# The two-input arithmetic of GpSimd goes to VectorE in a two-layer transformer trunk, and relu squared reads one factor from PSUM

## The chip, the cores and the metric

The kernel runs on one core of one Trainium2 chip. The metric is the device time of one execution in microseconds (us); lower is better. The engines are TensorE (PE), VectorE (DVE), ScalarE (ACT), GpSimd (POOL) and SyncE (SP, which here only issues DMAs). Each engine works through its own instruction stream in order, and waits on semaphores for the others.

## The reference

One sequence of 512 tokens with 1024 columns goes through two layers, all in fp32. A layer is, cut to what matters:

```
h = rmsnorm(x, norm_mix);  proj = h @ w_in                    # q, k, v, gates, u of three mixers
y_a = nsa_attention(...)   # 8 heads: compressed, full and window branches
y_b = banded_attention(...)  # window attention with sinks
y_c = s5_layer(u, ...)     # scan of a diagonal complex state, then gelu and a gate
merged = sum_i sigmoid(g_i) * (y_i @ w_branch_i)
x = x + merged @ w_out
h = rmsnorm(x, norm_mlp)
x = x + square(relu(h @ w_mlp_up)) @ w_mlp_down               # 4096 hidden columns
```

After the second layer one more rmsnorm gives the output.

## The kernel before

**Products in two parts.** Every fp32 operand of a large product is kept as a high part and a low part in the format fp32r, and a product is three matmuls: high by high, high by low, low by high (`mm3`, lines 143 to 145; `proj_tok`, line 563). A piece of weights (128 x 1024, 512 KB) is loaded by SP into `wr` (two buffers). `split` makes the two parts (three buffers each): ACT copies `wr` to the high part `wh` (line 136), and then VectorE or GpSimd subtracts to get the low part `wl` (line 137). Which of the two does it is the argument `eng`, None for VectorE.

**The stages of a layer.** The projections come first (with the first norm and the tables of the scan in layer 0), then the scan itself (`s5_quarter`, four quarters of 8 groups), then the attention, then the merge, `w_out`, and the MLP. In the attention the softmax work of one unit stands between the products of the unit before, and a generator `fill` feeds gate and branch products to TensorE in between. The MLP has four rounds (`fc`): eight up tiles (8 x 24 matmuls, one piece of weights each), then two column halves of the down product (four pieces each). For an up tile ACT takes the relu from its PSUM bank into `rel` (line 1348), VectorE squares it (line 1349), ACT copies the high part `ah` and VectorE subtracts the low part `al` (line 1350).

**The scan's tables.** `s5_prep` computes, by quarters, two tables with powers (`powers`, lines 497 to 499: a product on VectorE into `wpn` or `mo`, a product on GpSimd into `wpnt` or `mot`, and their sum on VectorE), the phasors `E`, and small matmuls (line 528) whose results VectorE adds into `ed` (line 532). The tables of layer 0 are made during its projections, those of layer 1 during the MLP of layer 0 (`steps` in `mlp`). The MLP of layer 1 has no such work beside it.

**Who sets the order.** The code states what depends on what and in which order things are wanted; a scheduling layer below it sets each engine's stream from that and from its own estimate of durations. So where an instruction stands changes when another one goes to another engine, and not only at the changed lines.

**GpSimd's arithmetic before.** The weights' low parts of layer 0's three first projections and of its whole MLP; those of the pieces that `fill` loads in both layers; one product of each table; the products with the sine and the back rotation in the scan (lines 741 and 749); the sums `merged` in `fill` (line 839); and the power -0.5 of each norm (line 230). GpSimd also issues the DMAs that store and load the scan's tables.

Of the kernel before, what the change touches and what calls it, by code (L numbers as in the profile page):

```python
# [28 lines left out]
# columns of the constant array  # L29
# [31 lines left out]
def bcast_rows(ap1d, n):  # L61
    """[n] in DRAM -> [128, n], the same row on every partition."""
    return bass.AP(tensor=ap1d.tensor, offset=ap1d.offset, ap=[[0, 128], [1, n]])


class Trunk:
# [14 lines left out]
    @contextmanager  # L81
    def after(self, pins):
        """What is emitted inside stays behind the given instructions in their engines' order."""
        with ExitStack() as s:
            for i in pins:
                s.enter_context(self.tc.issue_after(i.ins))
            yield

    # ---------------------------------------------------------------- background work
    def spawn(self, gen, delay=1):  # L90
        """Work cut into steps, set between the steps of the main line; a step yields how many of those to let pass."""
        item = [delay, gen]
        self.bg.append(item)
        return item
# [18 lines left out]
    # ---------------------------------------------------------------- psum  # L113
# [9 lines left out]
    # ---------------------------------------------------------------- weights  # L123
# [23 lines left out]
    # ---------------------------------------------------------------- constants  # L147
# [14 lines left out]
    def reduce_angle(self, pool, ang, n, name):  # L162
        """ang -> ang - 2 pi round(ang / 2 pi), in place."""
# [12 lines left out]
    def sincos(self, pool, ang, n, cos, sin, name):  # L176
        """cos and sin of ang in [-pi, pi]; ang is used up."""
# [28 lines left out]
    # ---------------------------------------------------------------- norm  # L206
    def norm_begin(self, p, row):
        """RMSNorm of self.x in two column halves: gain and the parts that a token tile takes."""
# [4 lines left out]
    def norm_sum(self, t, c, a=0, z=512):  # L213
        """Mean square of a token tile, after columns a to z of its half c are final (in their order)."""
# [32 lines left out]
    def norm_T(self, t):  # L247
        """Token tile t of the norm, transposed, in its two parts."""
# [4 lines left out]
    def norm_last(self, xg):  # L253
        """The norm of the last token tile, to be transposed by last_turn amid the work that follows."""
# [3 lines left out]
    def last_tile(self, b, mm, xg):  # L258
        """The last token tile's last columns in two parts, and its norm, brought out in the shortest time."""
# [32 lines left out]
    def first_norm(self, pa):  # L292
        """The first norm by token tiles, as a function that brings one up to its place in self.h, and the first
        pieces of weights that are loaded between the tiles."""
# [13 lines left out]
        # the tensor engine's clock rises only under load: keep it busy while the first tiles come  # L308
# [38 lines left out]
    # ---------------------------------------------------------------- S5 parameters  # L347
    def s5_init(self, l, p):
        """Powers of the discretised state matrix and its unit phasors, all groups at once."""
# [18 lines left out]
        # unit phasors of 8 * 2^k tokens, and of one  # L368
# [21 lines left out]
        # powers a^(8-e), e = 0..8  # L390
# [11 lines left out]
        # |a|^8  # L402
# [3 lines left out]
        # discretisation coefficient  # L406
# [17 lines left out]
    def s5_prep(self, l, init=None):  # L424
        """Tables of the chunked S5 scan (chunks of 8 tokens), by quarters of 8 groups, to DRAM."""
# [5 lines left out]
        with tc.tile_pool(name="prep", bufs=1, side="right", reuse_waits="tile") as p:  # L431
            pins.enter_context(self.after(self.pins))
            PR, PI, co_r, co_i, GC, GS, T1, T2, cmul = init[0] if init else list(self.s5_init(l, p))[1]
            # phasors of 8 b and of 64 a tokens, a, b < 8
# [12 lines left out]
            # the sine, which the imaginary half takes with the other sign  # L447
# [16 lines left out]
            for q in range(4):  # L464
# [8 lines left out]
                # B and C with their signs  # L473
# [15 lines left out]
                # tables with powers  # L489
                s4 = [128, 8, 8, 16]  # L490

                def powers(u, e0, name, sign=OP.add):
# [5 lines left out]
                    nc.gpsimd.tensor_tensor(tm, u2, pi, op=OP.mult)  # L498
# [4 lines left out]
                # phasors of the 64 chunks  # L503
# [18 lines left out]
                # the input table, transposed, and K[l] of the 8 lags, with d on lag 0  # L522
# [16 lines left out]
    # ---------------------------------------------------------------- projections to [token, column]  # L539
    def proj_tok(self, h, src, n, evac, stride=False, eng=None, lead=None, pre=()):  # L540
# [8 lines left out]
        for kp, t in order:  # L549
# [9 lines left out]
            # the low parts of the weights come last  # L559
# [8 lines left out]
    def resident(self, pool, src, n=4):  # L568
        """Pieces that all stay, as lists of [128, 512] parts per row tile."""
# [18 lines left out]
    def rope(self, pool, ps, t, out, shape):  # L588
        """ps [128, *heads, 64] -> rotated into out [128, *heads(, dup), 64]."""
# [14 lines left out]
    # ---------------------------------------------------------------- mixers  # L604
# [66 lines left out]
    def s5_u(self, l, h, p):  # L671
# [8 lines left out]
        self.proj_tok(h, self.I["wu"][l], 512, evac_u, stride=True, eng=None if l else self.nc.gpsimd)  # L680
# [21 lines left out]
    def s5_quarter(self, l, q, z, p):  # L702
        """The scan of 8 groups, over chunks of 8 tokens, up to the GLU's input."""
# [12 lines left out]
        # U[(s, h), group, chunk]  # L716
# [10 lines left out]
        # chunk inputs, rotated, scanned, rotated back  # L727
# [13 lines left out]
        nc.gpsimd.tensor_tensor(B, B, sinS, op=OP.mult)  # L741
# [4 lines left out]
        # the state before each chunk  # L746
        nc.gpsimd.memset(A[:, :, 0:1], 0.0)
        for k in (0, 64):
            nc.gpsimd.tensor_tensor(B[k:k + 64, :, 0:63], G[64 - k:128 - k, :, 0:63], sinS[64 - k:128 - k, :, 0:63], op=OP.mult)  # L749
# [17 lines left out]
    def glu(self, l, z, p):  # L767
# [14 lines left out]
        # the output takes the place of z  # L782
        for ct in range(4):
# [5 lines left out]
            # columns are (7 - j, c) of token 8 c + j  # L789
# [7 lines left out]
    def fill(self, l, h, yc, yb, merged, p, ng):  # L797
        for ct in range(ng, KT):
            yield from self.gate_first(l, 2, ct, h, merged, self.nc.gpsimd)
        yield from self.merge(l, 2, h, yc, merged, p, True, eng=self.nc.gpsimd)  # L800
# [256 lines left out]
    def b_parts(self, l, p, yb, t, hg):  # L1057
# [4 lines left out]
        P = []  # L1062
# [406 lines left out]
```

## Time and profile before

| | |
|---|---|
| median of 3 runs | 1933.46 us (1932.26 to 1934.83) |
| span of the profiled execution, first to last instruction | 1921.7 us |
| what lies around the span, against the median of the runs | 11.8 us |
| PE busy, share of the span | 1788.5 us, 93% |
| VectorE busy | 1156.1 us, 60% |
| ScalarE busy | 788.4 us, 41% |
| GpSimd busy | 428.4 us, 22% |

The profile is one execution on the chip. For it no time but its span is given; the three timed runs stand 11.8 us above that span at their median. Busy time is a mean over stages that have different limits, so each stage is read by itself. PE's busy time comes from modelled ends of matmuls; the granted clock says what share of the full TensorE clock was given.

### The profile page before, as it was taken

What the parts mean: (1) busy time and instruction counts of PE and PEld (TensorE: products, weight loads), DVE (VectorE), ACT (ScalarE), POOL (GpSimd) and SP (SyncE); (2) the same over time, 40 slices, a digit from 0 to 9 for tenths busy, and PEclk for the clock granted to TensorE, in tenths of its full rate; (3) what the DMA queues carried; (4) which work ended last, traced back from release to release, by engine and by line L of the source; (5) the groups of instructions that cost most, each with busy time, mean ns of one, the idle gap of its engine ahead of it and who ended that gap; (6) DMA issues with size and microseconds to landing.
All of it is one profiled execution on the core that took longest, in us unless ns stands there. A gap on an engine that the chain in (4) does not pass through costs nothing.

```text
span 1921.7 us, 23301 instructions
## 1 busy us (share of the span) xinstructions
PE 1788.5 (93%) x8560; PEld 1474.9 (77%) x8560; DVE 1156.1 (60%) x2552; ACT 788.4 (41%) x1575; POOL 428.4 (22%) x261
## 2 busy tenths in 40 slices
PE   7787989889999988989999999999899999999998
PEld 5776777677888866777787988777778888888887
DVE  7895558999345746355356456799954454334344
ACT  4422357666233323222334433776643333323232
POOL 4333421121202355455420032221230000000000
PEclk8898999999999999999999999999999999999999
DMA  5336421110333233333335353111132413333222
GB/s 165 112 131 178 143 68 56 33 45 23 134 102 119 64 102 107 119 110 109 123 110 158 111 154 110 55 45 34 34 109 90 141 59 96 99 99 99 94 95 86
DMA packets 66802, 188.23 MB, mean 98 GB/s; under 512 B 17984, under 2 KB 19168, under 8 KB 66688
## 3 DMA queue, kind: packets, MB, share of 16 engines
q1 hardware_dynamic: 57072, 156.53, 25.3%
q0 software_dynamic: 8320, 25.76, 4.4%
q10 hardware_dynamic: 1296, 4.46, 0.6%
q8 instruction: 67, 1.10, 0.2%
q14 instruction: 47, 0.39, 0.1%
HBM read 168.93 MB, written 17.76 MB: 97 GB/s over the span
## 4 chain that ended last, share of the span: by engine, by line
PE 59%; DVE 15%; issue 10%; POOL 4%; ACT 3%; DMA 1%; POOLq 0%; ACTq 0%; DVEq 0%
PE b_mm L144 16%; PE b_mm L145 16%; PE b_mm L143 16%; PE b_mm L563 3%; DVE aP L1212 3%; PE b_t L890 2%; POOL wl L137 1%; DVE ptl L897 1%; DVE aP L1199 1%; PE b_y L1121 1%; PE b_y L1119 1%; DVE rel L1349 1%; POOL sB L749 1%; POOL wpnt L498 1%; ACT wh L136 1%
## 5 line engine op out<-in xcount | busy, mean ns | idle before, releaser
L136 ACT CAST wh<-wr 128x1024 fp32r<-128x1024 f32 (+1 forms) x244 | 254.6, 1044 | 504.5 <-PE b_mm L144 233.4
L137 POOL TENSOR_TENSOR wl<-wr,wh 128x1024 fp32r<-128x1024 f32 (+1 forms) x112 | 276.2, 2468 | 541.5 <-ACT wh L136 426.8
L143 PE MATMUL b_mm<-hh,wh 128*128 128x512 f32 (+2 forms) x928 | 361.7, 390 | 0.5 <-ACT hh L290 0.5
L144 PE MATMUL b_mm<-hl,wh 128*128 128x512 f32 (+2 forms) x928 | 361.0, 389 | 0.6 <-DVE hl L290 0.6
L145 PE MATMUL b_mm<-hh,wl 128*128 128x512 f32 (+2 forms) x928 | 359.6, 387 | 0.3 <-POOL wl L137 0.3
L137 DVE TENSOR_TENSOR wl<-wr,wh 128x1024 fp32r<-128x1024 f32 (+1 forms) x132 | 164.6, 1249 | 281.4 <-ACT wh L136 281.2
L144 PEld LDWEIGHTS b_mm<-hl,wh 128*128 128x128 f32 x928 | 175.9, 190 | 33.4 <-DVE hl L290 1.1
L143 PEld LDWEIGHTS b_mm<-hh,wh 128*128 128x128 f32 x928 | 175.9, 190 | 33.1 <-ACT hh L290 1.0
L145 PEld LDWEIGHTS b_mm<-hh,wl 128*128 128x128 f32 x928 | 175.6, 189 | 33.2 <-POOL wl L137 1.2
L144 PE MATMUL b_mm<-wl,ah 128*128 128x512 f32 x448 | 176.0, 393 | 10.0 <-POOL wl L137 10.0
L143 PE MATMUL b_mm<-wh,ah 128*128 128x512 f32 x448 | 175.3, 391 | 0.0
L145 PE MATMUL b_mm<-wh,al 128*128 128x512 f32 x448 | 175.2, 391 | 0.0
L586 DVE TENSOR_TENSOR x<-b_mm,x 128x512 f32<-128x512 f32 x79 | 53.7, 688 | 114.2 <-PE b_mm L145 113.5
L563 PE MATMUL b_mm<-wh,hh 128*128 128x512 f32 (+1 forms) x320 | 108.6, 419 | 9.8 <-ACT v L982 4.7
L563 PE MATMUL b_mm<-wh,hl 128*128 128x512 f32 (+1 forms) x320 | 104.1, 403 | 7.5 <-DVE hl L290 7.5
L144 PEld LDWEIGHTS b_mm<-wl,ah 128*128 128x128 f32 x448 | 84.8, 189 | 29.3 <-POOL wl L137 11.6
L1349 DVE TENSOR_TENSOR rel<-rel 128x512 f32<-128x512 f32 x64 | 79.4, 1240 | 40.7 <-ACT rel L1348 40.7
L563 PE MATMUL b_mm<-wl,hh 128*128 128x512 f32 (+1 forms) x320 | 103.1, 402 | 0.3 <-DVE wl L137 0.3
L1350 ACT CAST ah<-rel 128x512 fp32r<-128x512 f32 x64 | 39.7, 621 | 148.5 <-DVE rel L1349 148.5
L145 PEld LDWEIGHTS b_mm<-wh,al 128*128 128x128 f32 x448 | 84.8, 189 | 17.6
L143 PEld LDWEIGHTS b_mm<-wh,ah 128*128 128x128 f32 x448 | 84.7, 189 | 17.7
L892 ACT CAST pth<-b_t 128x512 fp32r<-128x512 f32 x124 | 70.3, 585 | 66.4 <-PE b_t L890 66.0
(336 smaller groups left out, 3335.5 us busy)
## 6 DMA issues: line engine op xcount, KB each, us to landing
wr<-in_wup SPq DMA_DIRECT2D x64, 512.0 KB, 3.5
wr<-in_wdn SPq DMA_DIRECT2D x64, 512.0 KB, 3.5
wr<-in_wg SPq DMA_DIRECT2D x48, 512.0 KB, 3.5
wr<-in_wp SPq DMA_DIRECT2D x24, 512.0 KB, 3.5
wr<-in_wo SPq DMA_DIRECT2D x16, 512.0 KB, 3.6
x<-in_x SPq DMA_DIRECT2D x8, 512.0 KB, 6.6
wr<-in_wkv SPq DMA_DIRECT2D x8, 512.0 KB, 3.4
cw<-in_cw SPq DMA_DIRECT2D x16, 256.0 KB, 2.8
```

The costliest lines, as they stand in the source:

```text
L136: nc.scalar.copy(hi, raw)
L137: (eng or nc.vector).tensor_tensor(lo, raw, hi.bitcast(F32), op=OP.subtract)
L143: mm(out, ah, bh, start=start, stop=False)
L144: mm(out, ah, bl, start=False, stop=False)
L145: mm(out, al, bh, start=False, stop=stop)
L563: nc.tensor.matmul(banks[t][:, 0:n], part(a, kt, ts), w[b][:, k], start=kt == 0 and b == 0 and a is hh, stop=kt == KT - 1 and b == 1)
L586: self.nc.vector.tensor_tensor(o, bank, o, op=OP.add)
L890: nc.tensor.transpose(b[:, i * 128:(i + 1) * 128], x, self.ident)
L892: nc.scalar.copy(ph, b)
L1212: V.tensor_scalar(w, w, den[:, br, i:i + 1], g[:, br, i:i + 1], op0=OP.mult, op1=OP.mult)
L1349: nc.vector.tensor_tensor(r, r, r, op=OP.mult)
L1350: self.pins = (nc.scalar.copy(ah, r), nc.vector.tensor_tensor(al, r, ah.bitcast(F32), op=OP.subtract))
```

## The change

All `eng` arguments that named GpSimd become None, so that VectorE makes those low parts and sums; `powers`, line 741 and line 749 call VectorE instead of GpSimd; and line 1349 multiplies the PSUM bank with its relu instead of the relu with itself (the product is the same, since the relu is zero where the bank is negative). Comments and doc strings go too. Not changed: the power of the norm, one product in the last tile (line 262), and the low parts of the first two pieces of all (`lead` in `first_norm`), which stay on GpSimd.

```
@@ powers
-                    nc.gpsimd.tensor_tensor(tm, u2, pi, op=OP.mult)
+                    V.tensor_tensor(tm, u2, pi, op=OP.mult)
@@ s5_u (project_kv2 and project_kv01 alike)
-        self.proj_tok(h, self.I["wu"][l], 512, evac_u, stride=True, eng=None if l else self.nc.gpsimd)
+        self.proj_tok(h, self.I["wu"][l], 512, evac_u, stride=True, eng=None)
@@ s5_quarter
-        nc.gpsimd.tensor_tensor(B, B, sinS, op=OP.mult)
+        V.tensor_tensor(B, B, sinS, op=OP.mult)
...
-            nc.gpsimd.tensor_tensor(B[k:k + 64, :, 0:63], G[64 - k:128 - k, :, 0:63], sinS[64 - k:128 - k, :, 0:63], op=OP.mult)
+            V.tensor_tensor(B[k:k + 64, :, 0:63], G[64 - k:128 - k, :, 0:63], sinS[64 - k:128 - k, :, 0:63], op=OP.mult)
@@ fill
-            yield from self.gate_first(l, 2, ct, h, merged, self.nc.gpsimd)
-        yield from self.merge(l, 2, h, yc, merged, p, True, eng=self.nc.gpsimd)
+            yield from self.gate_first(l, 2, ct, h, merged, None)
+        yield from self.merge(l, 2, h, yc, merged, p, True, eng=None)
...
-        yield from self.merge(l, 1, h, yb, merged, p, eng=self.nc.gpsimd)
+        yield from self.merge(l, 1, h, yb, merged, p, eng=None)
@@ mlp (the pieces of wdn alike)
-                        parts = [(self.piece(I["wup"][l, fc * 8 + g], 8, 128, None if last else nc.gpsimd), self.bank("mm")) for g in two]
+                        parts = [(self.piece(I["wup"][l, fc * 8 + g], 8, 128, None), self.bank("mm")) for g in two]
...
-                    nc.vector.tensor_tensor(r, r, r, op=OP.mult)
+                    nc.vector.tensor_tensor(r, b, r, op=OP.mult)
```

The first place is the end of the second quarter of layer 1's tables, which are made in the MLP of layer 0. This is VectorE's stream before; `E` and `Et` are the quarter's phasors, `mo` its second table, `ed` its diagonal terms, `rel`, `ah` and `al` the activations of the up tiles of the second round:

```order
L514 TENSOR_TENSOR Et_6523<-PH_5806 128x512
L1349 TENSOR_TENSOR rel_6567<-rel_6567 128x512
L515 TENSOR_TENSOR E_6522<-E_6522,Et_6523 128x512
L497 TENSOR_TENSOR mo_6670<-ZI_5840,PR_5758 128x1024
L1350 TENSOR_TENSOR al_6569<-rel_6567,ah_6568 128x512
L1349 TENSOR_TENSOR rel_6605<-rel_6605 128x512
L1350 TENSOR_TENSOR al_6607<-rel_6605,ah_6606 128x512
L1349 TENSOR_TENSOR rel_6643<-rel_6643 128x512
L532 TENSOR_TENSOR ed_5991<-ed_5991,b_t_6651 128x48
```

GpSimd's stream before at that quarter, where `wl_6615`, `wl_6679` and `wl_6717` are the low parts of the weights for the up tiles 5, 6 and 7 of that round, counted from 0:

```order
L137 TENSOR_TENSOR wl_6615<-wr_6612,wh_6614 128x1024
L498 TENSOR_TENSOR wpnt_6518<-XX_6510,PI_5759 128x1024
L137 TENSOR_TENSOR wl_6679<-wr_6676,wh_6678 128x1024
L516 DMA cs11_6506<-E_6522 128x1024
L137 TENSOR_TENSOR wl_6717<-wr_6714,wh_6716 128x1024
L137 TENSOR_TENSOR wl_6759<-wr_6756,wh_6758 128x1024
L498 TENSOR_TENSOR mot_6671<-bc_5989,PI_5759 128x1024
```

VectorE's stream of the changed kernel at the same place:

```order
L514 TENSOR_TENSOR Et_6523<-PH_5806 128x512
L1349 TENSOR_TENSOR rel_6567<-b_mm_6542,rel_6567 128x512
L515 TENSOR_TENSOR E_6522<-E_6522,Et_6523 128x512
L1349 TENSOR_TENSOR rel_6605<-b_mm_6580,rel_6605 128x512
L1350 TENSOR_TENSOR al_6569<-rel_6567,ah_6568 128x512
L497 TENSOR_TENSOR mo_6670<-ZI_5840,PR_5758 128x1024
L1350 TENSOR_TENSOR al_6607<-rel_6605,ah_6606 128x512
L137 TENSOR_TENSOR wl_6679<-wr_6676,wh_6678 128x1024
L1349 TENSOR_TENSOR rel_6643<-b_mm_6618,rel_6643 128x512
L532 TENSOR_TENSOR ed_5991<-ed_5991,b_t_6651 128x48
L137 TENSOR_TENSOR wl_6717<-wr_6714,wh_6716 128x1024
```

What GpSimd did beside VectorE now stands in VectorE's one stream: the low part `wl_6679` comes behind the whole table work of the quarter, and behind the first product of the second table. The low part ahead of it in that stream is `wl_6615`, which stands before the quarter's first instruction; up to there TensorE can be served with tiles up to number 5.

The second place is the attention of layer 0, full branch of the second token tile. VectorE before, where `am` holds the maxima and sums, `aP` the scores, `aPc` those of the compressed blocks, `avy` and `yal` the result of the unit before:

```order
L858 TENSOR_TENSOR avy_3443<-b_y_3301,avt_3442 64x256 x2
L1166 TENSOR_REDUCE am_3397<-aPc_3398 128x4
L1199 ISA aP_3519,am_3397<-b_s_3516,consts_105 128x256
L1199 ISA am_3397 128x1
L1138 TENSOR_SCALAR am_3397<-am_3397 128x4
L862 TENSOR_TENSOR yal_2866<-avy_3443,yah_2865 128x2x128
L1139 RECIPROCAL am_3397<-am_3397 128x4
```

VectorE in the changed kernel, at the same place:

```order
L858 TENSOR_TENSOR avy_3443<-b_y_3301,avt_3442 64x256 x2
L1166 TENSOR_REDUCE am_3397<-aPc_3398 128x4
L137 TENSOR_TENSOR wl_3499<-wr_3496,wh_3498 128x1024
L862 TENSOR_TENSOR yal_2866<-avy_3443,yah_2865 128x2x128
L1138 TENSOR_SCALAR am_3397<-am_3397 128x4 x2
L137 TENSOR_TENSOR wl_3506<-wr_3503,wh_3505 128x1024
L1139 RECIPROCAL am_3397<-am_3397 128x4 x2
```

Low parts of weights now stand between the steps of a softmax. From the first score of an attention to its last scaled probability VectorE's stream has 14 of them and 4 sums `merged`, in either layer; before, GpSimd's had as many in that time.

## Rows read from the trace of the kernel before

**Rows 1.** Busy time by stretch, whole core: us, then each engine's, PE clock, DMA.
```profile
0.00:275.00 275.00, 225.83 (x1078) 190.35 (x1078) 192.85 (x434) 104.43 (x216) 97.15 (x81) 0.89 0.45 138
275.00:472.50 197.50, 177.94 (x944) 141.30 (x944) 182.96 (x585) 136.37 (x354) 39.00 (x18) 0.99 0.12 37
...
632.00:1010.00 378.00, 350.34 (x1555) 288.32 (x1555) 196.91 (x295) 112.12 (x161) 171.59 (x74) 0.97 0.33 107
...
1217.00:1411.00 194.00, 175.93 (x945) 139.24 (x944) 180.91 (x586) 136.47 (x354) 39.31 (x19) 1.00 0.12 39
...
1572.00:1922.00 350.00, 341.69 (x1549) 284.39 (x1547) 146.55 (x196) 106.89 (x148) 3.49 (x5) 1.00 0.29 95
```

**Rows 2.** Line 1349, the two MLPs' stretches apart: duration ns min/median/max, first and last start.
```profile
L1349 DVE TENSOR_TENSOR rel<-rel x32: 672/2483/2856, 635.3 to 977.4; 128x512 f32<-128x512 f32 x32
...
L1349 DVE TENSOR_TENSOR rel<-rel x32: 682/684/686, 1575.5 to 1871.9; 128x512 f32<-128x512 f32 x32
```

**Rows 3.** TensorE's waits in 632 to 1010 us: total us, times, longest.
```profile
PE b_t L528 <- DVE ed L532: 14.1, 5, 8.9
PE b_mm L144 <- POOL wl L137: 10.0, 4, 4.8
PE b_t L528 <- DVE wpn L499: 3.6, 1, 3.6
```

**Rows 4.** Chain that ended last: start, us, and what; then line 528 by itself.
```profile
733.52 1.00 PE b_t L528 x6
...
L528 PE MATMUL b_t<-ZI,wpn x64: 284/286/606, 729.3 to 940.1; 128*128 128x144 f32 x64
```

**Rows 5.** Timeline of GpSimd and VectorE in the second quarter's tables.
```profile
751.48 4.01 POOL L498 TENSOR_TENSOR wpnt<-XX,PI 128x1024 f32<-128x1024 f32 x1 [3.61 <-DVE XX L488]
...
755.52 3.40 DVE L499 TENSOR_TENSOR wpn<-wpn,wpnt 128x1024 f32<-128x1024 f32 x1 [1.94 <-POOL wpnt L498]
...
767.08 2.08 DVE L1350 TENSOR_TENSOR al<-rel,ah 128x512 fp32r<-128x512 f32 x1 [0.68 <-ACT ah L1350]
769.08 2.82 DVE L1349 TENSOR_TENSOR rel<-rel 128x512 f32<-128x512 f32 x1
```

**Rows 6.** Line 137 on both engines, and line 586: duration ns min/median/max.
```profile
L137 DVE TENSOR_TENSOR wl<-wr,wh x132: 1007/1225/3084, 129.1 to 1877.2; 128x1024 fp32r<-128x1024 f32 x128, 128x816 fp32r<-128x816 f32 x4
...
L137 POOL TENSOR_TENSOR wl<-wr,wh x112: 1927/2392/3681, 11.6 to 1432.2; 128x1024 fp32r<-128x1024 f32 x108, 128x816 fp32r<-128x816 f32 x4
...
L586 DVE TENSOR_TENSOR x<-b_mm,x x79: 677/691/692, 592.2 to 1908.0; 128x512 f32<-128x512 f32 x79
```

**Rows 7.** Timeline of VectorE and GpSimd at two places of layer 0's attention.
```profile
406.30 3.81 DVE L1212 TENSOR_SCALAR aP<-aP,am,gates 128x384 f32<-128x384 f32 x4
...
407.10 2.40 POOL L137 TENSOR_TENSOR wl<-wr,wh 128x1024 fp32r<-128x1024 f32 x1 [4.56 <-ACT wh L136]
...
420.30 1.63 DVE L1212 TENSOR_SCALAR aP<-aP,am,gates 128x384 f32<-128x384 f32 x4
```

**Rows 8.** Groups in 275 to 472.5 us: count, busy us, mean ns; then line 1142 by itself.
```profile
L1212 DVE TENSOR_SCALAR aP<-aP,am,gates 128x384 f32<-128x384 f32 x16 | 11.6, 777 | 0.0
...
L1212 DVE TENSOR_SCALAR aP<-aP,am,gates 128x512 f32<-128x512 f32 x15 | 10.4, 741 | 0.1
...
L1212 DVE TENSOR_SCALAR aP<-aP,am,gates 128x256 f32<-128x256 f32 x16 | 9.7, 651 | 0.0
...
L1142 DVE TENSOR_SCALAR am<-am 128x4 f32<-128x4 f32 x24 | 7.8, 328 | 0.1
...
L1142 DVE TENSOR_SCALAR am<-am x48: 136/160/2208, 334.1 to 1400.0; 128x4 f32<-128x4 f32 x48
```

**Rows 9.** Waits in 275 to 472.5 us: total us, times, longest.
```profile
PE b_y L1121 <- DVE ptl L897: 9.9, 7, 2.8
```

**Rows 10.** VectorE's waits in 0 to 250 us.
```profile
DVE sA L751 <- POOL sB L749: 6.7, 4, 2.5
...
DVE sA L742 <- POOL sB L741: 2.1, 2, 1.4
```

More of the change, by code (lines that the diff above doesn't have):

```diff
@@ L959, in turn @@
                 yield 1
-        self.proj_tok(h, self.I["wkv2"][l], 408, evac, eng=None if l else nc.gpsimd)
+        self.proj_tok(h, self.I["wkv2"][l], 408, evac, eng=None)
         self.spawn(turn(), 6)
@@ L993, in turn @@
             yield from self.compress(l, p)
-        self.proj_tok(h, self.I["wkv01"][l], 512, evac, eng=None if l else nc.gpsimd, lead=lead, pre=pre)
+        self.proj_tok(h, self.I["wkv01"][l], 512, evac, eng=None, lead=lead, pre=pre)
         self.cmp = self.spawn(turn(), 2)
@@ L1356, in mlp @@
                     for kp in range(4):
-                        w = self.piece(I["wdn"][l, fc, cc, kp], 2, 512, None if last else nc.gpsimd)
+                        w = self.piece(I["wdn"][l, fc, cc, kp], 2, 512, None)
                         for t in range(TT):
```

## The prediction

> **What bounds the kernel now.** I read the busy time of each engine by stretch first [rows 1]. TensorE is the bound where nothing disturbs it: in the MLP of layer 1 (1572 to 1922 us) it is busy 341.7 of 350 us at the full clock, while VectorE has 146.6 us of work. The MLP of layer 0 (632 to 1010 us) does the same products and takes longer. In the two attentions VectorE is all but full (183.0 of 197.5 us and 180.9 of 194.0) and TensorE waits for it, 18 to 20 us in each. The first 275 us have no single bound: TensorE is busy 225.8 us at 0.89 of its clock.
>
> Then I set the two MLPs beside each other by line 1349, the square of the relu. Its 32 squares start over 342.1 us in layer 0 (635.3 to 977.4) and over 296.4 us in layer 1 [rows 2]: 45.7 us more. The same row shows something else: one square takes 684 ns in layer 1, whatever the tile, and 2483 ns at the median in layer 0. The instruction and its data are of the same size. What differs is GpSimd, which is busy 171.6 us in the first of these stretches and 3.5 in the second [rows 1].
>
> The attention shows it in the open [rows 7]. Four scalings of 128 x 384 took 1.63 us at 420.30, with GpSimd idle, and 3.81 us at 406.30, when a GpSimd subtraction began among them at 407.10 and ran 2.40 us. So VectorE was held for 2.18 us, about as long as GpSimd worked. Not every instruction is held: line 586, which adds a PSUM bank to an SBUF tile, took between 677 and 692 ns in all 79 executions [rows 6].
>
> **The change part by part.** Moved to VectorE are 106 low parts of 1024 columns, 4 of 816, 16 table products, 24 scan products and 16 sums. A low part takes 2392 ns on GpSimd and 1225 ns on VectorE, medians [rows 6]. VectorE gets 106 x 1.23 + 4 x 1.01 + 16 x 1.22 (a table product is as large as a low part) + 8 x 0.69 + 16 x 0.68 + 16 x 0.69, together 181 us (a product of 512 columns costs about the 684 ns of a square), and is no longer held. I sum the effect by stage.
>
> *MLP of layer 0.* The 45.7 us have three parts. The tables of layer 1 need TensorE itself: line 528 has 64 matmuls at 1.00 us for 6 [rows 4], so 10.7 us that stay. Three waits make 14.1 + 10.0 + 3.6 = 27.7 us [rows 3]. The rest, 7.3 us, goes with a granted clock of 0.97 at the mean against 1.00, which is 2.4 GHz [rows 1]: for some stretches it stood at the lower level of 1.2 GHz. In the second quarter one sees what is late [rows 5]: the GpSimd product `wpnt` takes 4.01 us, the sum on VectorE waits 1.94 us for it and then takes 3.40 (2.2 more than 1.22), `al` is held for 2.08 us and the next square for 2.82, and behind these stands `ed`, for which TensorE waited 8.9 us, the longest wait in this stage. With the product on VectorE (1.22) and no holds this chain is shorter by 4.01 - 1.22 = 2.8 (in this the 1.94 of waiting is contained), 2.2, 1.4 and 2.1, in all 8.5 us: nearly the whole wait.
>
> The other side is the order. In the changed stream `wl_6679` stands behind the quarter's table work. Without holds I put this work at 12.7 us from the ready inputs on (before: 751.48 to 767.08, 15.6 us [rows 5], less the 1.94 waited and the 2.2 held, plus 1.22 for `wpnt`), and 2 us for the eight small steps ahead of it, estimates from those rows. TensorE meanwhile has three pieces ready, of 24 matmuls each at 350/1549 = 0.226 us [rows 1]: 16.3 us. So the low part is in time by about 1.6 us less its own 1.2: just. The 10.0 us of waits for low parts should go. What stays is a short wait for `ed` in each quarter, since the second batch of line 528 needs the one bank that ACT and VectorE must read first; I put 1.7 us on each (14.1 less the long one of 8.9 leaves 5.2 for four waits, 1.3 each, and VectorE has more queued), and 2 us for the first quarter, where the initial tables crowd VectorE. Gain: 27.7 + 7.3 - 4 x 1.7 - 2 = **26 us**. Its bounds are 35 (all waits and clock loss) and nothing (the waits move from GpSimd's low parts to VectorE's).
>
> *Attentions.* Added to VectorE in each: 14 x 1.23 + 4 x 0.69 = 20.0 us. Taken away is what it was held. The scalings of 384 columns were busy 11.6 us for 16, where 16 x 0.41 = 6.5 would do (the pace of 1.63 us for 4); those of 512 and 256 columns 20.1 us for 31, and 12.7 at that pace, which is too slow for the narrower and too fast for the wider; line 1142 took 7.8 us for 24 at a median of 0.16, so 3.8 [rows 7, 8]. These make 5.1 + 7.4 + 4.0 = 16.5, and other small steps are alike in part; at most it is GpSimd's 39.0 us of busy time [rows 1]. I take 23, near the lower end, because held time was seen only where such steps met GpSimd. So VectorE's load falls by 3 us per attention, and as it is the full engine there, the stage by about as much: **2 x 3 us**. Bounds: 20 slower (nothing given back) and 10 faster (the wait for `ptl`, 9.9 us [rows 9], gone).
>
> Here the Trainium skill speaks against the change. "Perfetto Trace Analysis", section Optimizing Scalar/DVE Operations, says that where DVE is saturated, offloading work to ScalarE or even GpSimd may make sense, and adds that the two share an SBUF read port, so that it might not help. By its first half the attention is the place to keep work on GpSimd, and each would lose the 20.0 us; by the held scalings the second half decides. I go by the rows.
>
> *First 275 us.* VectorE waited 6.7 + 2.1 us for GpSimd in the scan [rows 10]; the scan's product and two back rotations become shorter there. Against it the 9 + 4 low parts, tables and scan products add about 33 us to an engine with 192.9 of 275 us busy. No row prices the sum; it lies between 12 faster and 10 slower, and I take **3 us** faster. In layer 1's scan the same makes **1 us**.
>
> *At nothing.* The square from PSUM: 691 ns for the line 586 of equal size with one PSUM operand, against 684 [rows 2, 6]. Its bank is freed by VectorE instead of ACT, later by a square; seven banks cover that, unless VectorE falls behind by more than two tiles in a down product. The sums and low parts after 472 us: TensorE covers them there. GpSimd's DMAs lose what stood ahead of them.
>
> Sum: 26 + 6 + 3 + 1 = 36 us. The profiled span of 1921.7 becomes 1886; with the 11.8 us around it **1897.5 us** as a median, 1.9% faster.
>
> **Rivals.**
> 1. *VectorE's queue takes the place of GpSimd's* in layer 0's MLP: a low part misses its time behind each quarter's tables, by 4 to 5 us four times, and the clock falls with it. For it speaks that the margin above is under 2 us; against it that squares held to 2.5 us had filled the same queue. The gain of 26 shrinks to 8: 1915.
> 2. *The saturated engine decides* (the page's first half as a mechanism here): the held time in the attentions overlapped idle time, and the 20.0 us come on top in each. Then 26 + 4 - 40, 10 us slower: 1943. It decides from 15 us per attention on. VectorE's idle time there is only 14.5 us [rows 1], which speaks against it; the trace bears it out so far nowhere.
> 3. *More comes back*: all waits and clock loss of the MLP (35), 10 in each attention, 9 at the start: 64 us, 1869.
>
> **How the numbers follow.** I give the forecast (1880 to 1911) 0.58, rival 1 0.18, rival 2 0.08, rival 3 0.12, and 0.04 to no change that can be told. A measurement of this kernel can tell about 0.2%, 4 us. Faster are the first, second and fourth, 0.88; slower rival 2, 0.08. The range from 1868 to 1920 takes in the forecast, rivals 1 and 3, and leaves out less than 2 in 10.
>
> **What would show it.** Squares at 0.68 us in both MLPs; line 1142 never over 0.3 us; no wait of TensorE for a low part in 632 to 1010 us, and under 9 us for `ed` and `wpn`; the first MLP's squares within 320 us; VectorE's busy time up by far less than 181 us, to 1200 to 1250. Wrong would be: waits of TensorE for VectorE's `wl` of over 10 us in the first MLP (rival 1), or attentions longer than before (rival 2).

## The result, and the profile after

The changed kernel takes 1879.3 us as a median of 4 runs (1868.6 to 1880.8), the kernel before 1933.0 beside it (1932.3 to 1934.8): a ratio of 0.972, with a 95% interval of 0.969 to 0.975. The profiled execution of after ran 1880.8 us, its span is 1879.0; against the profiled execution of before that is 42.7 us less.

The windows of after over nearly the stretches of [rows 1], in order the start, the attention of layer 0, its MLP, the attention of layer 1 and its MLP. Columns: us, then busy time of PE, PEld, DVE, ACT and POOL with their counts, TensorE's granted clock, DMA share, GB/s.

```profile
0.00:264.00 264.00, 220.72 (x1082) 185.52 (x1083) 194.45 (x473) 102.62 (x215) 30.77 (x48) 0.90 0.48 145
264.00:460.00 196.00, 187.31 (x964) 147.22 (x963) 178.56 (x603) 137.65 (x357) 0.00 (x0) 0.97 0.12 39
617.00:934.00 317.00, 308.48 (x1387) 254.84 (x1387) 192.04 (x331) 101.60 (x139) 4.33 (x8) 0.99 0.38 116
1177.00:1376.00 199.00, 189.90 (x979) 149.19 (x980) 181.57 (x610) 138.60 (x359) 0.00 (x0) 0.97 0.14 43
1531.00:1829.00 298.00, 298.00 (x1330) 247.37 (x1330) 122.95 (x142) 93.48 (x119) 0.00 (x0) 1.00 0.31 97
```

GpSimd's column is empty in both attentions and in the second MLP. These windows differ a little in length from those of [rows 1]; cut at the same instructions as the table below, VectorE's busy time fell from 188.3 to 183.4 us in layer 0's attention and from 186.4 to 184.3 us in layer 1's, with 20 us of work more in each. For the whole program the page of after gives this:

```profile
PE 1789.9 (95%) x8560; PEld 1474.1 (78%) x8560; DVE 1178.3 (63%) x2718; ACT 786.9 (42%) x1574; POOL 58.8 (3%) x95
```

The lines that answer to [rows 2, 3]: the squares of after in either MLP (duration ns min/median/max, first and last start), then TensorE's waits in 617 to 934 us (total, times, longest).

```profile
L1349 DVE TENSOR_TENSOR rel<-b_mm,rel x32: 681/684/717, 618.8 to 935.0; 128x512 f32<-128x512 f32 x32
...
L1349 DVE TENSOR_TENSOR rel<-b_mm,rel x32: 681/683/684, 1533.7 to 1830.1; 128x512 f32<-128x512 f32 x32
```

```profile
PE b_mm L144 <- DVE wl L137: 5.1, 2, 2.7
PE b_mm L145 <- DVE wl L137: 1.7, 1, 1.7
PE b_t L528 <- DVE ed L532: 1.7, 1, 1.7
```

The squares cost the same in both MLPs now, and 27.7 us of waits have become 8.5. Those that answer to [rows 6, 8]: line 1142 (a clamp and negation of 128x4) and line 137 of after, then the scalings of line 1212 in 264 to 462 us (count, busy us and mean ns, idle before).

```profile
L1142 DVE TENSOR_SCALAR am<-am x48: 137/159/172, 319.3 to 1366.5; 128x4 f32<-128x4 f32 x48
...
L137 DVE TENSOR_TENSOR wl<-wr,wh x242: 999/1225/1250, 28.9 to 1835.3; 128x1024 fp32r<-128x1024 f32 x117, 128x816 fp32r<-128x816 f32 x4
```

```profile
L1212 DVE TENSOR_SCALAR aP<-aP,am,gates 128x512 f32<-128x512 f32 x16 | 7.6, 540 | 0.0
L1212 DVE TENSOR_SCALAR aP<-aP,am,gates 128x384 f32<-128x384 f32 x16 | 7.0, 472 | 0.0
L1212 DVE TENSOR_SCALAR aP<-aP,am,gates 128x256 f32<-128x256 f32 x16 | 5.7, 406 | 0.0
```

The longest of 48 steps of line 1142 fell from 2208 to 172 ns, the longest low part on VectorE from 3084 to 1250, and three widths of the scalings from 31.7 us (47 instructions) to 20.3 (48).

To see where the time came from, I cut four profiled executions at the same instructions: the first transpose of the queries (line 871), the last product with v, the first and the last relu of an MLP (line 1348). "Again" is the kernel before in a second execution, "small loads" the last version of the experiments below.

| us | before | again | after | small loads | predicted change |
|---|---|---|---|---|---|
| start, to the first transpose of queries | 270.7 | 268.6 | 259.8 | 260.0 | -3 |
| attention, layer 0 | 209.1 | 207.1 | 204.2 | 204.2 | -3 |
| to the first relu | 154.9 | 154.9 | 153.5 | 153.5 | 0 |
| MLP, layer 0 | 342.1 | 342.0 | 316.2 | 316.2 | -26 |
| norm, projections, scan of layer 1 | 236.4 | 242.6 | 241.1 | 231.1 | -1 |
| attention, layer 1 | 206.2 | 208.6 | 204.1 | 204.0 | -3 |
| to the first relu | 154.9 | 154.9 | 153.5 | 153.5 | 0 |
| MLP, layer 1 | 296.5 | 296.5 | 296.5 | 296.5 | 0 |
| to the end | 51.0 | 51.0 | 50.1 | 50.1 | 0 |

### The profile page after: what moved, and what is told of

Same layout as the page of the kernel before. It is cut to its first block, busy times and chain, and to the rows that moved or that the text cites. A ratio compares the mean times of both kernels' runs of the same rounds, so it can differ in the third digit from the quotient of the medians.

```text
span 1879.0 us, 23205 instructions
## 1 busy us (share of the span) xinstructions
PE 1789.9 (95%) x8560; PEld 1474.1 (78%) x8560; DVE 1178.3 (63%) x2718; ACT 786.9 (42%) x1574; POOL 58.8 (3%) x95
## 5 line engine op out<-in xcount | busy, mean ns | idle before, releaser
L137 DVE TENSOR_TENSOR wl<-wr,wh 128x1024 fp32r<-128x1024 f32 (+1 forms) x242 | 293.9, 1216 | 396.4 <-ACT wh L136 396.3
L563 PE MATMUL b_mm<-wh,hl 128*128 128x512 f32 (+1 forms) x320 | 102.9, 399 | 11.2 <-DVE hl L290 11.1
L145 PEld LDWEIGHTS b_mm<-wh,al 128*128 128x128 f32 x448 | 84.6, 189 | 17.6
L143 PEld LDWEIGHTS b_mm<-wh,ah 128*128 128x128 f32 x448 | 84.4, 188 | 17.6
L563 PEld LDWEIGHTS b_mm<-wh,hl 128*128 128x128 f32 x320 | 66.9, 219 | 21.4 <-DVE hl L290 13.2
L897 DVE TENSOR_TENSOR ptl<-b_t,pth 128x512 fp32r<-128x512 f32 x108 | 72.8, 686 | 16.0 <-ACT pth L892 15.2
L563 PEld LDWEIGHTS b_mm<-wh,hh 128*128 128x128 f32 x320 | 64.7, 219 | 19.3 <-ACT hh L290 3.4
```

Of the source, the lines that this page charges most:

```text
L137: (eng or nc.vector).tensor_tensor(lo, raw, hi.bitcast(F32), op=OP.subtract)
L143: mm(out, ah, bh, start=start, stop=False)
L145: mm(out, al, bh, start=False, stop=stop)
L563: nc.tensor.matmul(banks[t][:, 0:n], part(a, kt, ts), w[b][:, k], start=kt == 0 and b == 0 and a is hh, stop=kt == KT - 1 and b == 1)
L897: nc.vector.tensor_tensor(pl, b, ph.bitcast(F32), op=OP.subtract)
```

## The experiments

My theory was that VectorE is held while GpSimd works, so that work taken from GpSimd gives back more than it costs. Its rivals were that GpSimd's results simply came late, and that a saturated VectorE would pay for the work.

**Where the first MLP's 26 us come from.** Three kernels take one piece each; the ratios of all experiments are to the kernel before, measured beside them.

The square's factor alone, in the kernel before:

```diff
-                    nc.vector.tensor_tensor(r, r, r, op=OP.mult)
+                    nc.vector.tensor_tensor(r, b, r, op=OP.mult)
```

> The kernel before with one line changed: the square of the relu takes one factor from its PSUM bank; all GpSimd work stays. Theory 'held' (GpSimd instructions hold VectorE's SBUF operands): the 32 squares of the first MLP fall from a median of 2.48 us to 0.69, but the hold partly falls on the next VectorE instruction with SBUF operands; the first MLP's squares then start over 325 to 338 us instead of 342.1, all else as before, 4 to 17 us faster. Rival 'late product' (GpSimd's low parts and products are only slow themselves, the holds cost nothing): squares shorter, but the time within 4 us of before.

Measured: 1918.7 us, ratio 0.994 (0.992 to 0.995), so 12 us faster; the MLP 327.5 us. TensorE's waits in it fell from 27.7 to 13.3 us. Line 1349 and line 1350 of this kernel in 630 to 970 us (busy us, mean ns):

```profile
L1350 DVE TENSOR_TENSOR al<-rel,ah 128x512 fp32r<-128x512 f32 x32 | 37.3, 1166 | 16.1 <-ACT ah L1350 16.1
L1349 DVE TENSOR_TENSOR rel<-b_mm,rel 128x512 f32<-128x512 f32 x32 | 22.0, 688 | 51.3 <-ACT rel L1348 51.3
```

And of the kernel before:

```profile
L1349 DVE TENSOR_TENSOR rel<-rel 128x512 f32<-128x512 f32 x32 | 57.5, 1797 | 40.7 <-ACT rel L1348 40.7
L1350 DVE TENSOR_TENSOR al<-rel,ah 128x512 fp32r<-128x512 f32 x32 | 29.5, 923 | 16.0 <-ACT ah L1350 16.0
```

With GpSimd as busy as before, a square that takes one factor from PSUM is not held at all (688 ns), and 35.5 us come back; 7.8 of them go to the subtraction behind it, which still has two SBUF inputs and meets the same GpSimd work.

GpSimd makes the same low parts in the same queue in this kernel, in 2460 ns each against 2505, so these 12 us are not the price of its slowness.

The low parts of layer 0's MLP alone, in the kernel before:

```diff
-  parts = [(self.piece(I["wup"][l, fc * 8 + g], 8, 128, None if last else nc.gpsimd), self.bank("mm")) for g in two]
+  parts = [(self.piece(I["wup"][l, fc * 8 + g], 8, 128, None), self.bank("mm")) for g in two]
...
-  w = self.piece(I["wdn"][l, fc, cc, kp], 2, 512, None if last else nc.gpsimd)
+  w = self.piece(I["wdn"][l, fc, cc, kp], 2, 512, None)
```

> The kernel before, with only the low parts of the first MLP's weights on VectorE; the tables' products and the square as before. Theory 'held': the 57 low parts are most of GpSimd's work there, so the first MLP's squares start over 316 to 324 us (316.2 in the changed kernel, 342.1 before), 18 to 26 us faster in all. Rival 'the tables' products are what was late' (the chain through wpnt): no more than 10 us faster.

Measured: 1911.3 us, ratio 0.990 (0.988 to 0.993), 19 us faster; the MLP 325.1 us, just over the 316 to 324 expected, all squares under 0.71 us. The last kernel is the changed one with the square back on SBUF alone:

```diff
-                    nc.vector.tensor_tensor(r, b, r, op=OP.mult)
+                    nc.vector.tensor_tensor(r, r, r, op=OP.mult)
```

> The changed kernel, but the square of the relu reads SBUF twice as before. Theory 'held': with GpSimd idle nothing is held, squares at 0.68 us in both MLPs, time within 4 us of the changed kernel. Rival (the PSUM factor carries a part of the gain by itself): 8 us or more slower than the changed kernel.

Measured: 1873.7 us, ratio 0.970 (0.967 to 0.973), the MLP 316.2 us, as in the changed kernel. So the factor from PSUM is worth 12 us beside a busy GpSimd and nothing beside an idle one: it is a second way to the same gain. The two single edits together would make 14.6 + 17.0 = 31.6 us in this MLP, and the whole change makes 25.9. A few microseconds of this can't be settled by one profile: with the same code and nearly the same waits this MLP took 347.2 us instead of 342.1 in the profile of the next experiment, at a granted clock of 0.96 against 0.97, and 319.4 instead of 316.2 in the two last tests of the holding below, at 0.98 against 0.99.

**The attention.** The low parts and sums of the attention's fill alone, in the kernel before:

```diff
-            yield from self.gate_first(l, 2, ct, h, merged, self.nc.gpsimd)
-        yield from self.merge(l, 2, h, yc, merged, p, True, eng=self.nc.gpsimd)
+            yield from self.gate_first(l, 2, ct, h, merged, None)
+        yield from self.merge(l, 2, h, yc, merged, p, True, eng=None)
...
-        yield from self.merge(l, 1, h, yb, merged, p, eng=self.nc.gpsimd)
+        yield from self.merge(l, 1, h, yb, merged, p, eng=None)
```

> The kernel before, with only the low parts and sums of the attention's fill on VectorE. Theory 'held': attention with its merge 3 to 6 us shorter in each layer (6.3 and 3.5 us in the changed kernel), all else as before, 6 to 12 us faster. Rival 'saturated engine' (the added 20.0 us of VectorE work lands on the end): each attention 10 us or more longer, 20 us or more slower in all.

Measured: 1915.1 us, ratio 0.992 (0.989 to 0.995), 16 us faster, more than the 6 to 12 expected. The attentions took 202.9 and 202.5 us against 206.2 to 209.1, and the start 264.2 against 268.6 and 270.7, since some of these pieces are split there too. VectorE's load in layer 0's attention, 20 us of new work included, is 178.74 of 196 us (before: 182.96 of 197.5), POOL's 0.00:

```profile
270.00:466.00 196.00, 187.35 (x964) 147.19 (x962) 178.74 (x596) 136.58 (x356) 0.00 (x0) 0.97 0.12 41
```

The saturated engine did not decide, because the load fell.

**The start.** Two kernels take one edit each into the kernel before: the low parts of layer 0's three first projections, and the tables' products.

```diff
-        self.proj_tok(h, self.I["wkv2"][l], 408, evac, eng=None if l else nc.gpsimd)
+        self.proj_tok(h, self.I["wkv2"][l], 408, evac, eng=None)
```

(`wkv01` and `wu` alike.)

> The kernel before, with only the low parts of layer 0's three first projections on VectorE. The changed kernel's first stage (to the first transpose of attention's queries) took 259.8 us against 268.6 and 270.7 in two executions of before, where 3 us had been forecast. Theory: half of it is from these low parts: VectorE's rope and low-part work at 60 to 110 us was held by them (2.16 us for a scaling of 0.28). Then the first stage takes 263 to 267 us, the total is 3 to 8 us under before's. Rival: the tables alone set it; first stage and total as before within 2 us.

```diff
-                    nc.gpsimd.tensor_tensor(tm, u2, pi, op=OP.mult)
+                    V.tensor_tensor(tm, u2, pi, op=OP.mult)
```

> The kernel before, with only the tables' products of line 498 on VectorE. Theory: the other half of the first stage's gain is from them: TensorE waited for line 499 behind GpSimd's product (4.3 us at 151 us), and line 499 was held (3.4 us against 1.23). Then the first stage takes 262 to 267 us, and the first MLP, whose tables are the same code, 336 to 342 us against 342; the total is 3 to 10 us under before's. Rival: the queue of VectorE is full there (45.4 of 51.2 us), the products only add to it, and the first stage is as long as before or up to 4 us longer.

The first: 1926.1 us, ratio 0.996 (0.994 to 0.999), the start 265.2 us. The second: 1940.1 us, ratio 1.002 (1.000 to 1.004), so that its time can hardly be told from before's; the start 267.8 us and the MLP of layer 0 351.3 us, 9 longer than in before's two profiles. TensorE's waits of the second in 632 to 985 us:

```profile
PE b_t L528 <- DVE ed L532: 13.5, 5, 5.2
PE b_mm L144 <- POOL wl L137: 9.0, 3, 5.2
PE b_mm L143 <- ACT wh L136: 5.4, 1, 5.4
PE b_mm L145 <- POOL wl L137: 4.2, 1, 4.2
```

Here my forecast failed, and the trace of this kernel shows how. In before VectorE paused 1.94 us for GpSimd's product in the second quarter's tables [rows 5]. Now it makes that product itself and runs through the table work without a pause and at full pace, and the one that is held is GpSimd. Its low part that began at 749.80 us ended at 765.03, when VectorE's string of work had ended at 762.8. GpSimd's two low parts from there (duration ns min/median/max, first and last start), then three instructions of VectorE's string (start us, duration us):

```profile
L137 POOL TENSOR_TENSOR wl<-wr,wh x2: 2361/8796/15232, 749.8 to 765.0; 128x1024 fp32r<-128x1024 f32 x2
```

```profile
751.33 1.22 DVE L498 TENSOR_TENSOR wpnt<-XX,PI 128x1024 f32<-128x1024 f32 x1
753.52 1.22 DVE L499 TENSOR_TENSOR wpn<-wpn,wpnt 128x1024 f32<-128x1024 f32 x1
762.15 0.68 DVE L1350 TENSOR_TENSOR al<-rel,ah 128x512 fp32r<-128x512 f32 x1
```

TensorE waited 4.2 us for the low part that took 15.23 us. In two other quarters two low parts took 16.2 and 17.6 us together, where 4.8 would do. So holding goes both ways, and moving the products alone hands the loss to GpSimd's low parts; how much of the 9 us this makes is not shown, since the clock is lower too (0.95 against 0.97). Once the low parts are off GpSimd the same edit gains: 325.1 us with the low parts moved, 316.2 with both (the square adds nothing there, as shown above). Part by part the start gives 2, 4 and 5 us (products, projections, fill, each against the mean of 268.6 and 270.7, which differ by 2 themselves); the whole change got 10.

**What holds VectorE.** The direct test adds GpSimd work to the changed kernel that computes nothing that is used, so that only the meeting of the engines is left. In a first try it stood behind each weight piece of the first MLP:

```diff
+                    nc.gpsimd.tensor_copy(junk[:, 416:417], w[0].rearrange("p a b -> p (a b)")[:, 0:1].bitcast(F32))
+                    for _ in range(3):
+                        nc.gpsimd.tensor_tensor(junk[:, 0:416], junk[:, 0:416], junk[:, 0:416], op=OP.mult)
```

> The changed kernel, with work on GpSimd in the first MLP that nobody waits for: behind each weight piece a one-column copy and three two-input products of 128x416 on a buffer of their own in SBUF, about as much busy time as the low parts took before (some 60 x 3 us against 60 x 2.39). Theory: what cost in the first MLP was that VectorE's instructions with two SBUF inputs are held while GpSimd runs one. Then those subtracts of VectorE (line 1350, line 137, and the table products) go from 0.69 and 1.23 us up to 1 to 3 us, the squares, which take one input from PSUM, stay at 0.69, and the MLP goes from 316 us to 322 to 340; total 6 to 24 us slower than the changed kernel. Rival: what cost was only that GpSimd's low parts came late (2.39 us each, in its queue); nobody waits for this work, so the MLP stays at 316 us and the total within 3 us of the changed kernel.

The control has `for _ in range(5): nc.gpsimd.memset(junk[:, 0:416], 0.0)` in place of the products.

> As the run with the products, but behind each weight piece GpSimd fills its buffer five times (128x416, no input read) in place of the products. Theory: holding needs two-input work on both engines; fills leave VectorE's subtracts at 0.69 and 1.23 us, the MLP at 315 to 318 us and the total within 3 us of the changed kernel. Rival: any access of GpSimd to SBUF holds VectorE, and the MLP is as long as with the products.

Measured: 1992.1 us with products (ratio 1.031, 1.028 to 1.034), the MLP 427.0 us; 1895.7 with fills (0.981, 0.979 to 0.984), the MLP 333.6. Both are far from what either theory said, and the reason is in the waits of the run with products, 613 to 1040 us:

```profile
ACT wh L136 <- POOL junk L1331: 127.1, 12, 16.6
```

The one-column copy reads a weight buffer, so the buffer came free only when GpSimd got to it, and ACT waited 127.1 us for that, 14.8 us with the fills. "Nobody waits for it" was wrong. VectorE was also busy 238.1 us there against 192.0 in after, and its low parts took 1359 ns beside the products and 1223 beside the fills, so that holding had a part, but these two runs can't size it. The second try ties nothing: 60 products of 128x1024 in the second MLP, on a buffer of their own, and 120 fills as a control.

```diff
+            if last:
+                junk = p.tile([128, 1024], F32, name="junk")
+                nc.gpsimd.memset(junk, 0.0)
+                for _ in range(60):
+                    nc.gpsimd.tensor_tensor(junk, junk, junk, op=OP.mult)
```

> The changed kernel, with 60 two-input products of 128x1024 on GpSimd in the second MLP, on a buffer of their own in SBUF: as many and as large as the low parts that the first MLP had on GpSimd before. The runs with work behind each weight piece tied a weight buffer's release to GpSimd; here no instruction of another engine waits for GpSimd or is waited for by it, and its own next work is the last norm. Theory: an instruction of VectorE with two SBUF inputs is held for the rest of the GpSimd product that it meets. Then line 137 goes from 1.23 to 2.5 to 3.6 us and line 1350 from 0.69 to 1.5 to 3 us for as long as the products run (140 to 250 us), line 1349, with a factor from PSUM, stays at 0.68, and the MLP goes from 296.5 us to 300 to 325, since 3.6 + 0.7 + 2.6 us by piece are more than TensorE's 5.45. Rival: the engines don't hold each other; all three lines and the 296.5 us stay.

> As the run with the products in the second MLP, but with 120 fills of 128x1024 on GpSimd, which read nothing. Theory: no holding; lines 137, 1349 and 1350 stay at 1.23, 0.68 and 0.69 us, the second MLP at 296.5 us, the total within 3 us of the changed kernel. Rival: GpSimd's mere use of SBUF holds VectorE, and lines 137 and 1350 lengthen as with the products.

Lines 137, 1350 and 1349 (here 1355 and 1354) in the 143 us in which the products ran (busy us, mean ns, idle before):

```profile
L137 DVE TENSOR_TENSOR wl<-wr,wh 128x1024 fp32r<-128x1024 f32 x27 | 60.5, 2242 | 40.5 <-ACT wh L136 40.5
L1355 DVE TENSOR_TENSOR al<-rel,ah 128x512 fp32r<-128x512 f32 x16 | 16.2, 1012 | 11.0 <-ACT ah L1355 11.0
L1354 DVE TENSOR_TENSOR rel<-b_mm,rel 128x512 f32<-128x512 f32 x16 | 10.9, 678 | 0.0
```

The same with the fills:

```profile
L137 DVE TENSOR_TENSOR wl<-wr,wh 128x1024 fp32r<-128x1024 f32 x27 | 33.1, 1225 | 71.1 <-ACT wh L136 71.1
L1355 DVE TENSOR_TENSOR al<-rel,ah 128x512 fp32r<-128x512 f32 x16 | 11.1, 693 | 11.0 <-ACT ah L1355 11.0
L1354 DVE TENSOR_TENSOR rel<-b_mm,rel 128x512 f32<-128x512 f32 x16 | 10.9, 684 | 0.0
```

This settles the mechanism: of the two kinds of GpSimd work only the products, which read SBUF, hold VectorE, and only the two instructions with two SBUF inputs are held among these three. The Trainium skill says the same of such instructions ("SBUF — State Buffer", section Who interferes with whom): two SBUF inputs contend with a GpSimd instruction that reads SBUF, not with one that only writes it. The runs agree, 2242 against 1225 ns. My price was wrong, though: the MLP took 296.4 us with the products and 296.5 with the fills, and the totals are those of the changed kernel (1877.2 and 1876.6 us, ratios 0.970). VectorE was held for 32 us (87.6 against 55.1 in these three lines) and idled 31 less before line 137. TensorE did not notice, as the window of the run with products shows:

```profile
1537.00:1680.00 143.00, 143.00 (x639) 118.66 (x639) 92.62 (x70) 44.30 (x58) 133.31 (x56) 1.00 0.31 100
```

VectorE is busy 92.62 of 143 us there, held time included: without tables in its queue that MLP has room for it, and being held was free there.

**The stretch behind the first MLP.** It was 4.7 us longer in after than in before, against a forecast of 1 us less. I ran the kernel before once more, unchanged.

> The kernel before once more, unchanged, for its profile. The profiled execution of before had a span of 1921.7 us, while the spans of its other executions lie 1.8 us under their times (1925.4 to 1936.0). Theory: that execution was an early one; its stretch between the first MLP and layer 1's attention (236.4 us, against 239 to 243 in all the other kernels run, changed there or not) was short because two small loads landed early, for which VectorE waits (line 1011 4.9 us, line 773 0.2 us) ahead of the low part hl for which TensorE waits (1.6 us). Then this execution has a span of 1925 to 1935, that stretch 239 to 244 us and the wait for hl in it 4 to 8 us. Rival: the stretch is 236 us here too, and the 4.7 us that the changed kernel lost there come from its scan products on VectorE.

Its span is 1926.1 us, the stretch 242.6 us, and TensorE's wait for `hl`, the low part of the normed activations, is 6.3 us against 1.6 in the first execution of before and 7.4 in after. So this wait comes and goes in one and the same code. VectorE's timeline in after shows what has (start us, duration us, idle before):

```profile
983.08 1.42 DVE L240 SCALAR_TENSOR_TENSOR xgl<-x,nst,gainb 128x512 f32<-128x512 f32 x2
984.47 0.17 DVE L1051 MEMSET vcst<- 128x128 f32 x1
994.97 0.18 DVE L1011 COPY ck<-cpos 128x16 f32<-128x16 f32 x1 [10.34 <-DMA cpos<-in_cpos]
996.24 0.17 DVE L773 TENSOR_SCALAR gb<-gb 128x4 f32<-128x4 f32 x1 [1.09 <-DMA gb<-in_glub]
996.31 1.28 DVE L290 TENSOR_TENSOR hl<-b_y,hh 128x512 fp32r<-128x512 f32 x2
```

Two instructions on 8 and 2 KB of data stand ahead of `hl`, for which TensorE waits, and their loads are issued among four tables of 512 KB. One edit takes them out of the way: the two small buffers come from the pool that lives through the program, so their loads are issued near its start.

```diff
-        gb = p.tile([128, 4], F32, name="gb")
+        gb = self.cp.tile([128, 4], F32, name=f"gb{l}")
...
-            pos = p.tile([128, 16], F32, name="cpos", tag="cpos", bufs=2)
+            pos = self.cp.tile([128, 16], F32, name=f"cpos{l}{j}")
```

> The changed kernel, with two kinds of small loads (128x16 compress positions, 128x4 GLU biases) in buffers of their own from the pool that lives through the program, so that both layers' loads are issued in the first 60 us instead of beside the scan tables of 0.5 MB. Theory: in layer 1 VectorE waits for them 7 to 13 us ahead of the low part for which TensorE waits (7.4 us in the changed kernel's profile, with the granted clock at 0.90 in the 50 us after). Then that wait falls under 2 us, the stretch between the MLP and layer 1's attention from 241 to 231 to 236 us, and the total is 4 to 10 us under the changed kernel's. Rival: TensorE would wait for hl just the same, since the norm behind it is what is late; stretch and total unchanged within 2 us.

Measured: 1869.2 us (1866.5 to 1871.0), ratio 0.967 (0.965 to 0.969), the best of all kernels here, though its interval touches the changed kernel's (0.969 to 0.975). The stretch takes 231.1 us at a granted clock of 1.00, against 238.3 to 241.1 in the six profiles that have the changed kernel's code there, and `hl` follows its own inputs:

```profile
983.31 1.42 DVE L240 SCALAR_TENSOR_TENSOR xgl<-x,nst,gainb 128x512 f32<-128x512 f32 x2
984.71 0.17 DVE L1051 MEMSET vcst<- 128x128 f32 x1
988.64 1.29 DVE L290 TENSOR_TENSOR hl<-b_y,hh 128x512 fp32r<-128x512 f32 x2 [3.77 <-ACT hh L290]
```

No wait of TensorE for `hl` of over 0.2 us is left in it, and the other stretches of this kernel agree with after's within 0.2 us.

## Why the prediction was right, and where it was not

The direction and the mechanism were right. The forecast was 1897.5 us and the time is 1879.3, 18 us lower, just under the range that I gave the likeliest case (1880 to 1911) and nearer to rival 3's 1869. By stage the MLP and the attentions came out near the forecast, and the start as in rival 3. Step by step:

- *MLP of layer 0: -26 forecast, -25.9 measured.* The sum is right, two of its terms are not: 8.8 us of waits were to stay, all for `ed`, and 8.5 stayed, but 6.8 of them for low parts in VectorE's queue and only 1.7 for `ed`. That 8.5 lies so near 8.8 is luck. So rival 1's mechanism is there, at 6.8 us instead of 18. That TensorE would not wait for low parts any more was wrong: the margin, 1.6 us less the low part's own 1.2, was too thin. The 4.01 us of `wpnt`, too, were not GpSimd's own pace (the product `mot` of equal size took 2.04) but the same holding, by VectorE's lines 497 and 510.
- *Attentions: -3 each forecast; -3.9 and -3.3 against the mean of the two executions of before.* VectorE's busy time fell by 4.9 and 2.1 us, where 3 were forecast, so that with the 20.0 us added 24.9 and 22.1 of being held went away; I had taken 23. The stretches behind them gave another 1.4 each, which I had put at nothing. Rival 2 fell with the fill alone.
- *Start: -3 forecast, -9 to -11 measured.* This is the term that was mis-sized. I had priced the scan's waits and nothing for held instructions, although the start had GpSimd busy 97 of 275 us. VectorE's busy time up to the first transpose is 192.1 us before and 192.2 after, with an estimated 33 us of work more, so about as much holding went away there. The longest scaling of line 477 in before took 2156 ns where 280 is the median:

```profile
L477 DVE TENSOR_SCALAR ZI<-bc,consts x8: 272/280/2156, 62.0 to 876.8; 128x128 f32<-128x128 f32 x8
```

  The rule that I applied to the attention should have been applied there too.
- *Norm, projections and scan of layer 1: -1 forecast, +4.7 on the profiles.* The two small loads make this stretch vary by 6 us in one and the same kernel (236.4 and 242.6), and the execution of before that I summed against had them early. Over the profiles of all kernels with before's code there it takes 236.4 to 242.7 us, with the changed code 238.3 to 241.1, so no effect of the scan's products can be told.
- *The 11.8 us around the span.* This step was wrong. In later executions the span lies 1.8 us under the time (1926.1 of 1927.9, 1879.0 of 1880.8). So the profiled execution of before took about 1923.5 us, some 9.5 less than the median; I had taken this difference for something outside the span. 6.2 us of it are the stretch with the small loads; the rest I can't place.
- *VectorE's busy time: 1200 to 1250 us forecast, 1178.3 measured.* It took on 181 us and rose by 22, so that about 159 us of being held went away (an estimate, 181 less 22), more than I had dared to count.
- *The square from PSUM at nothing*: right for the changed kernel, where it meets no GpSimd work; the experiment shows what it is worth where it does.

That 42.7 us lie between the two profiles and 53.7 between the medians is no contradiction: before's profiled execution was some 9.5 us under its median, after's 1.5 over. The profiles of the experiments narrow it. Over all executions in which a stage's code was as in before (four to seven of them) and as in after (four to seven), the means differ by 11.2 us in the start, 5.5 and 4.5 in the attentions, 25.6 in the first MLP, 1.0 in layer 1's norm, projections and scan, and 2.9 in the rest. That makes 50.7 us, inside the 49 to 60 that the interval of the ratio gives. Open stays why single executions of before range from 1925 to 1943 us; the small loads show 6 us of this, and the first MLP 5 more at a lower granted clock.

## What to carry to other kernels

Before work is shared between VectorE and GpSimd, look for one instruction of VectorE whose duration differs by stretch; if it is long exactly where GpSimd reads SBUF, the shared work is paid for on the engine that it was to relieve, and moving all of it back may gain where moving a part of it gains nothing. An operand taken from PSUM is the cheap way out where GpSimd must stay busy. And look at what stands in an engine's queue ahead of the instruction for which TensorE waits: a load of a few KB that is issued beside large ones is worth moving to the start.

## What the runs showed of the hardware

- A load of 8 KB issued at 982.46 us in after, among four tables of 512 KB issued from 979.65 to 983.67, was waited for until 994.97: 12.5 us. In the second execution of before VectorE waited 8.8 us for the same load, in the first 4.9. Nothing in the code differs between the latter two.
- Being held can cost nothing: 32 us of it in the second MLP left TensorE busy for all 143 us of the window.
- The holding goes both ways: beside a string of VectorE's instructions without a pause one low part on GpSimd took 15.23 us, where 2.39 is the median.
- Instructions with one tensor input are not all spared. Line 1142, of one tensor of 128x4 in SBUF, took up to 2208 ns in before and at most 172 in after, where GpSimd is idle in the attentions. The Trainium skill ("SBUF — State Buffer", the same section) names this form among those that can take both ports.
